# Retention's gates and values: the last additions of each column pair as accumulating transfers, and one more row pair by 7 products

## The chip, the cores and the metric

The kernel runs on one core of one Trainium2 chip. The metric is device time in microseconds of one execution. The core's engines are TensorE (PE, with its weight loads shown apart as PEld), VectorE (DVE), ScalarE (ACT), GpSimd (POOL) and SyncE (SP); SP, ACT and POOL also issue DMA transfers, each in its own queue and in order.

## What is computed

A decoder trunk of two layers, float32, for 256 rows of 2048 features. The first layer is a retention layer followed by a squared-ReLU MLP, the second a latent-attention layer followed by another such MLP. The change touches the retention layer:

```python
def retention(h, w_in, w_out, cos, sin):
    proj = h @ w_in
    q, k, v, gate = jnp.split(proj, [H * dk, 2 * H * dk, 2 * H * dk + H * dv], axis=-1)
    q = apply_rope(...); k = apply_rope(...) * (dk ** -0.5)
    ...
    o = o_intra + o_cross
    o = o * lax.rsqrt(jnp.mean(o * o, axis=-1, keepdims=True) + RMS_EPS)
    return (jax.nn.silu(gate) * o) @ w_out
```

There are 8 heads; a head's q and k are 256 wide, its v and its gate 512 wide. `h` is the normed input. The kernel scales by the norm's gain on the way in and by each row's factor (`r0`) only after the product.

## The kernel before

**Tiles and products.** Every float32 operand is split into a high part and a low part (`split`, lines 180 to 189: a copy on ACT, then a subtraction on DVE), and a product is three matmuls, high by high, high by low and low by high (lines 352 to 354). Weights come in chunks of 128 x 2048 through a pool of three `raw` tiles; their parts go to pools of five `wh` and five `wl` tiles. Activations stand ready as split tiles (`act0`, one for each of 8 pairs of 128 features).

**Row pairs and products.** `gemm_pair` (line 329) makes a 256 x 1024 result from 8 row pairs, one `quad` each (line 280). A quad is a 2 x 2 block product. By 8 products it needs the raw weights' two splits only. By 7 products it also needs sums of the activations (`sums0`, from `with_sums`) and sums of the weights (`us`, three DVE additions at lines 312 to 317), which are split too. `kinds` says which pairs take 7: `SEVEN = (3, 5, 7)` or `FOUR = (3, 5, 6, 7)` (lines 47 and 48). FOUR is in use already in the attention's output product (`wop`).

**After the products.** `pair_out` (line 364) copies six accumulators to SBUF tiles on ACT and adds two more on DVE. One step later `rest` makes two subtractions and hands four pairs of tiles on, whose sums are the blocks of the result: (c11, p1), (c12, v), (c21, u), (c22, p5). `summed` (line 381) adds each pair on DVE (line 385).

**Order.** The program is unrolled, and the order of work around the products is written by hand: `later(n, fn)` puts `fn` off by n chunks, `tick` counts chunks, `need` runs waiting work until a tile exists. A planner then orders each engine's instructions by this priority and by what is ready in its own estimate, and gives out buffers. All 512-wide SBUF tiles that are neither weights nor activations (`f2k`, line 72) share 14 buffers, among them the gates, the values, q and k, the score tiles and the input tiles `x0t`.

**Heads.** For head 1 to 7 (lines 728 to 766) come q (stage `rq`, 2 chunks), k (`rk`, 2 chunks), then gate and value together as one column pair (`rp`, 8 chunks), whose results are taken up during the next head's `rq` and `rk`: `paired` (line 753) adds the pairs, passes the gate through Silu (line 756), and `ret_valued` (line 707) splits the value into vh and vl; `ret_out` (line 656) is put off by one chunk and multiplies scores with values, norms on POOL (lines 161 and 163), multiplies by the gate on DVE (line 672), and transposes y two chunks later. After head 3 and after head 7 a half of the output product follows (`ro`).

**Start.** `first_inputs` (line 571) loads a pair of x's transposed columns, `x0t`, splits it, and for the pairs in SEVEN keeps the tile, scales it again in `sum_up` 9 + c chunks later, and makes the sums of activations from it.

**Other accumulating transfers.** `to_home` (line 143) adds results to DRAM tiles `xh` with transfers issued by POOL (line 148).

Of the kernel before, what the change touches and what calls it, by code (L numbers as in the profile page):

```python
# [15 lines left out]
AF = mybir.ActivationFunctionType  # L16
ALU = mybir.AluOpType
# [19 lines left out]
NT = 2  # L37
S = NT * P
# [8 lines left out]
SEVEN = (3, 5, 7)  # L47
QUERY, FOUR = (3, 4, 6, 7), (3, 5, 6, 7)
PI = math.pi

G_MIX0, G_MLP0, G_KV, G_MIX1, G_MLP1 = 0, 16, 32, 48, 64
# [15 lines left out]
def yoco(ctx: ExitStack, tc: tile.TileContext, a):  # L67
    nc = tc.nc
# [3 lines left out]
    def f2k(shape, name, dtype=F32):  # L72
        return pool.tile([P, *shape], dtype, tag="f2k", bufs=14, name=name)
# [8 lines left out]
    def bank(tag, shape, name):  # L82
        t = psum.tile([P, 512], F32, tag=tag, bufs=4 if tag == "acc" else 2, name=name)
        return shaped(t, shape)

    def two_banks(name):
        return psum.tile([P, 2, 512], F32, tag="at", bufs=1, name=name)

    def act_tile(name, dtype=F32R):

        return pool.tile([P, 2, 2, S], dtype, tag="act", bufs=24, name=name)
# [5 lines left out]
    def later(n, fn):  # L97
        queue.append((clock[0] + n, next(count), fn))
# [6 lines left out]
    def tick():  # L105
        clock[0] += 1
        while queue and min(q[0] for q in queue) <= clock[0]:
            run_first()

    def need(items, n):  # L110
        while len(items) < n:
            run_first()
# [41 lines left out]
    def gain(col):  # L154
        return gains[:, col : col + 1]
# [24 lines left out]
    def split(h, l, src, scale=None):  # L180

        if scale is None:
            nc.scalar.copy(h, src)  # L183
            nc.vector.tensor_tensor(l, src, h.bitcast(F32), op=ALU.subtract)  # L184
        else:
            nc.scalar.activation(h, src, AF.Copy, scale=scale)
            nc.vector.scalar_tensor_tensor(
                l, src, scale, h.bitcast(F32), op0=ALU.mult, op1=ALU.subtract
            )

    def split_act(v, src, scales=(None, None)):
        if scales == (None, None):
            split(v[:, :, 0], v[:, :, 1], src)
        else:
            for j in range(2):
                split(v[:, j, 0], v[:, j, 1], src[:, j], scales[j])
# [132 lines left out]
    def gemm_pair(w, chunk0, act, kinds, name, done):  # L329

        made = {}
        total, count = {}, {}
        for seven in kinds:
            for key in ("c11", "c12", "c21"):
                total[key] = total.get(key, 0) + (1 if seven else 2)
            for key in ("p1", "p5", "p6", "p7") if seven else ("c22", "c22"):
                total[key] = total.get(key, 0) + 1

        def get(key):
            if key not in made:  # L340
                if key in ("p6", "p7"):
                    both = two_banks(f"{name}_p67")
                    made["p6"], made["p7"] = both[:, 0], both[:, 1]
                else:
                    made[key] = bank("tp" if key[0] == "p" else "acc", [512], f"{name}_{key}")
            return made[key]

        def mm(key, lhs, rhs):
            dst, n = get(key), count.get(key, 0)
            count[key] = n + 1  # L350
            (ah, al), (bh, bl) = lhs, rhs
            nc.tensor.matmul(dst, ah, bh, start=n == 0, stop=False)  # L352
            nc.tensor.matmul(dst, ah, bl, start=False, stop=False)  # L353
            nc.tensor.matmul(dst, al, bh, start=False, stop=n == total[key] - 1)  # L354

        for i in range(len(kinds)):
            need(act, i + 1)
            v, more = act[i]
            quad(w, chunk0 + i, (v, more if kinds[i] else None), mm, f"{name}{i}")
            if i == len(kinds) - 1:  # L360
                queue.append((clock[0] + 1, -1, lambda: pair_out(made, name, done)))
            tick()

    def pair_out(c, name, done):

        o = {}
        for key in ("c22", "c12", "c11", "c21", "p1", "p5"):
            o[key] = f2k([512], f"{name}_{key}")
            nc.scalar.copy(o[key], c[key])  # L369
        v, u = (f2k([512], f"{name}_{i}") for i in "vu")  # L370
        nc.vector.tensor_tensor(v, c["p6"], o["p1"], op=ALU.add)
        nc.vector.tensor_tensor(u, c["p7"], v, op=ALU.add)

        def rest():
            nc.vector.tensor_tensor(v, o["p5"], v, op=ALU.subtract)
            nc.vector.tensor_tensor(o["p5"], o["p5"], u, op=ALU.subtract)
            done([[(o["c11"], o["p1"]), (o["c12"], v)], [(o["c21"], u), (o["c22"], o["p5"])]])

        later(1, rest)

    def summed(c):

        for row in c:
            for block in row:
                nc.vector.tensor_tensor(block[0], block[0], block[1], op=ALU.add)
        return [[block[0] for block in row] for row in c]

    def with_sums(blocks, name):

        blocks = blocks.rearrange("p j (t n) -> p (j t) n", t=NT)  # L390
        sums = f2k([4, P], f"{name}_sum")
        nc.vector.tensor_tensor(sums[:, 0:2], blocks[:, 0:2], blocks[:, 1:4:2], op=ALU.subtract)
        nc.vector.tensor_tensor(sums[:, 2], sums[:, 1], blocks[:, 0], op=ALU.subtract)
        nc.vector.tensor_tensor(sums[:, 3], blocks[:, 2], sums[:, 2], op=ALU.add)
        more = act_tile(f"{name}_more")
        split_act(more, sums.rearrange("p (j t) n -> p j (t n)", j=2))
        return more
# [130 lines left out]
    scale = (NOPE + ROPE) ** -0.5  # L528
# [40 lines left out]
    act0, sums0, r0, ret_sc, mla_sc, no_turn = [], [], [], [], [], []  # L569

    def first_inputs(c):

        t = f2k([2, S], f"x0t_{c}")
        nc.sync.dma_start(t, a["xt"][:, 2 * c : 2 * c + 2, :])
        v = act_tile(f"a0_{c}")
        split_act(v, t, [gain(G_MIX0 + 2 * c + j) for j in range(2)])
        act0.append(v)
        sums0.append(None)
        if c in SEVEN:

            def sum_up():
                for j in range(2):
                    nc.scalar.activation(t[:, j], t[:, j], AF.Copy, scale=gain(G_MIX0 + 2 * c + j))
                sums0[c] = with_sums(t, f"a0s_{c}")

            later(9 + c, sum_up)

# [119 lines left out]
    def ret_valued(src, h, s, v, gate):  # L707
        for t in range(NT):
            vh = f2k([512], f"vh{h}{t}", F32R)
            vl = f2k([512], f"vl{h}{t}", F32R)  # L710
            split(vh, vl, src[t], r0[t])
            v.append((vh, vl))
        later(1, lambda: ret_out(h, s, v, gate, halves[h // 4]))
# [14 lines left out]
    for h in range(RH):  # L728
        qk, gate, v, s = [], [], [], []
        if h == 0:  # L730

            def gated(acc, gate=gate):
                src = [f2k([512], f"gate_raw{t}") for t in range(NT)]
                for t in range(NT):
                    nc.scalar.copy(src[t], acc[t])

                def silu():
                    for t in range(NT):
                        g = f2k([512], f"gate0{t}")
                        nc.scalar.activation(g, src[t], AF.Silu, scale=r0[t])  # L740
                        gate.append(g)

                later(8, silu)

            gemm(a["ret_w_gv0"], 0, act0, KD, 512, "rg0", gated, start)
            ret_projected(h, qk, gate, v, s)
            gemm(
                a["ret_w_gv0"], 4, act0, KD, 512, "rv0",
                lambda acc, v=v, s=s, gate=gate: ret_valued(acc, 0, s, v, gate),
            )  # L750
            continue

        def paired(c, h=h, gate=gate, v=v, s=s):
            c = summed(c)
            for t in range(NT):
                nc.scalar.activation(c[t][0], c[t][0], AF.Silu, scale=r0[t])
                gate.append(c[t][0])
            ret_valued([c[t][1] for t in range(NT)], h, s, v, gate)

        ret_projected(h, qk, gate, v, s)  # L760
        if h == RH // 2:
            ret_out_half(0)
        need(r0, NT)
        while None in [sums0[k] for k in SEVEN]:
            run_first()
        gemm_pair(a["ret_w_gv"], (h - 1) * 8, list(zip(act0, sums0)), [k in SEVEN for k in range(8)], f"rp{h}", paired)
    ret_out_half(1)


# [412 lines left out]
```

## Time and profile before

| | |
|---|---|
| median of 3 runs | 2503.48 us (2501.48 to 2504.06) |
| span of the profiled execution | 2497.0 us |
| weight loads on PE, busy | 2075.1 us, 83% |
| ACT busy | 1574.8 us, 63% |
| POOL busy | 252.2 us, 10% |
| transfers of the SP queue (q1) | 471.78 MB, 52.5% of 16 engines' span |
| transfers issued by POOL (q0) | 46.15 MB, 8.9% |

The profiled execution has a span of 2497.0 us from its first instruction to its last; the runs' time contains some more around it. A row of a timeline gives the start in us from the span's start, the duration in us, the engine, the line, the operation, the tiles (out<-in), the shapes and a count; in square brackets stands the idle time before it and what ended it. A row of groups ends with the busy time, the mean ns of one, and the idle time before them with its releasers. Matmuls overlap, so their rows are longer than the steps between them.

### The profile page before, as it was taken

The numbers are of one execution on the slowest core, as the hardware profiler recorded it, in microseconds if no ns is written. First come the engines' busy times: TensorE is split into PE (matmuls) and PEld (weight loads), VectorE is DVE, ScalarE is ACT, GpSimd is POOL, SyncE is SP. The second block draws the span as 40 slices with busy tenths as digits, with TensorE's granted clock in tenths as the row PEclk, the third lists the DMA queues.
The fourth block names the chain that finished last, engine by engine and source line by source line (L and its number), as shares of the span: only waits on it lengthen the run. The fifth ranks groups of instructions, "written<-read, shape, count | busy, mean of one in ns | idle before, by whom it ended". The sixth has DMA issues, their size and how long they took to land.

```text
span 2497.0 us, 31492 instructions
## 1 busy us (share of the span) xinstructions
PE 2471.9 (99%) x11683; PEld 2075.1 (83%) x11683; DVE 2096.7 (84%) x2723; ACT 1574.8 (63%) x2228; POOL 252.2 (10%) x308
## 2 busy tenths in 40 slices
PE   8999999999999999999999999999999999999999
PEld 7788888888888888888888888998888888888887
DVE  7788888888898888889889888776899888898896
ACT  6566555555676657566666767666676566575663
POOL 6300011000010110110110101110010201101100
PEclk9999999999999999999999999999999999999999
DMA  8545568555565685775875555444455956857754
GB/s 290 211 173 202 178 217 246 183 193 196 211 217 189 207 263 186 235 237 186 247 259 191 197 196 189 159 149 163 173 213 203 262 203 213 249 187 233 258 200 165
DMA packets 92825, 519.97 MB, mean 208 GB/s; under 512 B 11009, under 2 KB 12161, under 8 KB 39425
## 3 DMA queue, kind: packets, MB, share of 16 engines
q1 hardware_dynamic: 71280, 471.78, 52.5%
q0 software_dynamic: 21248, 46.15, 8.9%
q8 instruction: 91, 1.49, 0.2%
q14 instruction: 62, 0.50, 0.1%
q10 hardware_dynamic: 144, 0.05, 0.0%
HBM read 478.09 MB, written 39.85 MB: 207 GB/s over the span
## 4 chain that ended last, share of the span: by engine, by line
PE 80%; DVE 10%; DMA 4%; ACT 4%; issue 2%; POOL 1%; ACTq 0%; SPq 0%; DVEq 0%; POOLq 0%
PE u_c L353 7%; PE u_c L354 7%; PE u_c L352 7%; PE d_c L353 4%; PE d_c L354 4%; PE d_c L352 4%; PE rp_c L353 3%; PE rp_c L354 3%; PE rp_c L352 3%; DVE d_wl L184 3%; PE ro_c L352 2%; PE ro_c L353 2%; PE ro_c L354 2%; PE rq_acc L272 2%; PE rk_acc L272 2%; DMA d_raw<-in_mlp_w 2%
## 5 line engine op out<-in xcount | busy, mean ns | idle before, releaser
L184 DVE TENSOR_TENSOR u_wl<-u_raw,u_wh 128x1024 fp32r<-128x1024 f32 (+1 forms) x256 | 280.0, 1124 | 35.8 <-ACT u_wh L183 35.8
L184 DVE TENSOR_TENSOR d_wl<-d_raw,d_wh 128x1024 fp32r<-128x1024 f32 (+1 forms) x256 | 283.4, 1132 | 26.0 <-ACT d_wh L183 25.1
L353 PE MATMUL u_c<-u_wl,n 128*128 128x512 f32 x748 | 291.8, 390 | 1.1 <-DVE u_wl L184 1.0
L352 PE MATMUL u_c<-u_wh,n 128*128 128x512 f32 x748 | 291.3, 391 | 0.0
L354 PE MATMUL u_c<-u_wh,n 128*128 128x512 f32 x748 | 291.3, 389 | 0.0
L183 ACT CAST u_wh<-u_raw 128x1024 fp32r<-128x1024 f32 (+1 forms) x256 | 238.9, 981 | 60.6 <-DMA u_raw<-in_mlp_w 27.2
L183 ACT CAST d_wh<-d_raw 128x1024 fp32r<-128x1024 f32 (+1 forms) x256 | 240.0, 991 | 56.3 <-DMA d_raw<-in_mlp_w 25.1
L353 PE MATMUL d_c<-d_wl,hid 128*128 128x512 f32 x644 | 251.4, 390 | 1.7 <-DVE d_wl L184 1.6
L352 PE MATMUL d_c<-d_wh,hid 128*128 128x512 f32 x644 | 252.1, 391 | 0.0
L354 PE MATMUL d_c<-d_wh,hid 128*128 128x512 f32 x644 | 250.9, 390 | 0.0
L183 ACT CAST u_wh<-u_u 128x1024 fp32r<-128x1024 f32 x92 | 94.2, 1050 | 153.5 <-DVE u_u L317 129.8
L183 ACT CAST d_wh<-d_u 128x1024 fp32r<-128x1024 f32 x84 | 84.9, 1049 | 162.6 <-DVE d_u L317 154.7
L353 PEld LDWEIGHTS u_c<-u_wl,n 128*128 128x128 f32 x748 | 140.5, 188 | 31.1 <-DVE u_wl L184 2.8
L354 PEld LDWEIGHTS u_c<-u_wh,n 128*128 128x128 f32 x748 | 140.4, 188 | 29.2
L352 PEld LDWEIGHTS u_c<-u_wh,n 128*128 128x128 f32 x748 | 140.4, 188 | 28.6
L183 ACT CAST rp_wh<-rp_raw 128x1024 fp32r<-128x1024 f32 x112 | 106.7, 972 | 67.7 <-PE rp_c L354 37.5
L184 DVE TENSOR_TENSOR u_wl<-u_u,u_wh 128x1024 fp32r<-128x1024 f32 x92 | 110.7, 1222 | 43.6 <-ACT u_wh L183 43.5
L353 PEld LDWEIGHTS d_c<-d_wl,hid 128*128 128x128 f32 x644 | 120.9, 188 | 29.0 <-DVE d_wl L184 4.5
L354 PEld LDWEIGHTS d_c<-d_wh,hid 128*128 128x128 f32 x644 | 120.9, 188 | 25.1
L352 PEld LDWEIGHTS d_c<-d_wh,hid 128*128 128x128 f32 x644 | 120.9, 188 | 24.6
L184 DVE TENSOR_TENSOR d_wl<-d_u,d_wh 128x1024 fp32r<-128x1024 f32 x84 | 99.9, 1222 | 35.9 <-ACT d_wh L183 35.9
L148 POOL DMA_DIRECT2D xh<-d_c x48 | 42.1, 1029 | 844.6 <-ACT d_c L369 844.5
(567 smaller groups left out, 6570.0 us busy)
## 6 DMA issues: line engine op xcount, KB each, us to landing
u_raw<-in_mlp_w SPq DMA_DIRECT2D x128, 1024.0 KB, 5.3
d_raw<-in_mlp_w SPq DMA_DIRECT2D x112, 1024.0 KB, 4.9
rp_raw<-in_ret_w_gv SPq DMA_DIRECT2D x56, 1024.0 KB, 4.9
ro_raw<-in_ret_w_out SPq DMA_DIRECT2D x32, 1024.0 KB, 4.9
uq_raw<-in_mla_w_uq SPq DMA_DIRECT2D x24, 768.0 KB, 4.1
rq_raw<-in_ret_w_qk SPq DMA_DIRECT2D x16, 1024.0 KB, 6.6
rk_raw<-in_ret_w_qk SPq DMA_DIRECT2D x16, 1024.0 KB, 4.8
d_raw<-in_mlp_w2t SPq DMA_DIRECT2D x16, 1024.0 KB, 5.1
```

Of the source, the lines that this page charges most:

```text
L148: nc.gpsimd.dma_start(x_home[t][2 * p + j], part, accum_op=ALU.add)
L183: nc.scalar.copy(h, src)
L184: nc.vector.tensor_tensor(l, src, h.bitcast(F32), op=ALU.subtract)
L272: nc.tensor.matmul(acc[f], wh[:, cols], a.rearrange("p i s -> p (i s)"), start=k == 0, stop=k == nk - 1)
L352: nc.tensor.matmul(dst, ah, bh, start=n == 0, stop=False)
L353: nc.tensor.matmul(dst, ah, bl, start=False, stop=False)
L354: nc.tensor.matmul(dst, al, bh, start=False, stop=n == total[key] - 1)
```

## The change

The last additions of a retention head's column pair are issued as four transfers by POOL that accumulate from one SBUF tile into another, in place of four DVE additions; Silu, the split of the values and what follows come one chunk later. In the same stage the row pairs by 7 products are FOUR in place of SEVEN. The sums for these pairs are no longer made from the kept `x0t` tile: `sum_up` loads the columns once more into a tile of its own, for four pairs instead of three.

```diff
-        if c in SEVEN:
+        if c in FOUR:
 
             def sum_up():
+                again = f2k([2, S], f"x0s_{c}")
+                nc.sync.dma_start(again, a["xt"][:, 2 * c : 2 * c + 2, :])
                 for j in range(2):
-                    nc.scalar.activation(t[:, j], t[:, j], AF.Copy, scale=gain(G_MIX0 + 2 * c + j))
-                sums0[c] = with_sums(t, f"a0s_{c}")
+                    nc.scalar.activation(again[:, j], again[:, j], AF.Copy, scale=gain(G_MIX0 + 2 * c + j))
+                sums0[c] = with_sums(again, f"a0s_{c}")
...
         def paired(c, h=h, gate=gate, v=v, s=s):
-            c = summed(c)
-            for t in range(NT):
-                nc.scalar.activation(c[t][0], c[t][0], AF.Silu, scale=r0[t])
-                gate.append(c[t][0])
-            ret_valued([c[t][1] for t in range(NT)], h, s, v, gate)
+            for t, j in ((0, 0), (1, 0), (0, 1), (1, 1)):
+                nc.gpsimd.dma_start(c[t][j][0], c[t][j][1], accum_op=ALU.add)
+
+            def landed():
+                for t in range(NT):
+                    nc.scalar.activation(c[t][0][0], c[t][0][0], AF.Silu, scale=r0[t])
+                    gate.append(c[t][0][0])
+                ret_valued([c[t][1][0] for t in range(NT)], h, s, v, gate)
+
+            later(1, landed)
...
-        while None in [sums0[k] for k in SEVEN]:
+        while None in [sums0[k] for k in FOUR]:
             run_first()
-        gemm_pair(a["ret_w_gv"], (h - 1) * 8, list(zip(act0, sums0)), [k in SEVEN for k in range(8)], f"rp{h}", paired)
+        gemm_pair(a["ret_w_gv"], (h - 1) * 8, list(zip(act0, sums0)), [k in FOUR for k in range(8)], f"rp{h}", paired)
```

## The prediction

> **What bounds the kernel now.** I read the page first, then the timeline of TensorE in one steady stretch, then the busy time of one whole head.
>
> ```profile
> span 2497.0 us, 31492 instructions
> PE 2471.9 (99%) x11683; PEld 2075.1 (83%) x11683; DVE 2096.7 (84%) x2723; ACT 1574.8 (63%) x2228; POOL 252.2 (10%) x308
> PE 80%; DVE 10%; DMA 4%; ACT 4%; issue 2%; POOL 1%; ACTq 0%; SPq 0%; DVEq 0%; POOLq 0%
> ```
>
> ```profile
> 251.96 0.39 PE L352 MATMUL rp_c<-rp_wh,a 128*128 128x512 f32 x1
> ...
> 255.13 0.39 PE L354 MATMUL rp_c<-rp_wh,a 128*128 128x512 f32 x1
> ...
> 213.40:281.80 68.40, 68.40 (x338) 57.74 (x337) 57.42 (x75) 40.36 (x54) 1.83 (x4) 1.00 0.52 187
> ```
>
> TensorE (PE) sets the time: it is busy 99% of the span and carries 80% of the chain. The 0.39 us of a matmul's row is not its price, since the next one starts before it ends. From 251.96 to 255.13 there are 14 steps, so a matmul costs 3.17/14 = 0.227 us. In the second row (one head, from 213.40 us on: its columns are PE, weight loads, DVE, ACT, POOL) PE never stops for 68.40 us, at full clock, while DVE works 57.42 us and ACT 40.36. So matmuls taken away are worth their 0.227 us, and vector work costs nothing as long as DVE stays ahead.
>
> **The change, part by part.** *Matmuls removed.* In each of the seven paired heads, row pair 6 goes from 8 products to 7, and a product is 3 matmuls: 7 x 3 = 21 matmuls x 0.227 = -4.8 us. This is the whole direct gain.
>
> *Vector work added and removed.*
>
> ```profile
> L184 DVE TENSOR_TENSOR rp_wl<-rp_raw,rp_wh 128x1024 fp32r<-128x1024 f32 x91 | 107.7, 1220 | 6.7 <-ACT rp_wh L183 6.2
> L184 DVE TENSOR_TENSOR rp_wl<-rp_u,rp_wh 128x1024 fp32r<-128x1024 f32 x42 | 51.3, 1225 | 25.6 <-ACT rp_wh L183 25.5
> L312 DVE TENSOR_TENSOR rp_u<-rp_raw 128x1024 f32<-128x1024 f32 x21 | 25.6, 1221 | 11.4 <-DMA rp_raw<-in_ret_w_gv 11.4
> L316 DVE TENSOR_TENSOR rp_u<-rp_u,rp_raw 128x512 f32<-128x512 f32 x21 | 14.5, 689 | 0.4
> L317 DVE TENSOR_TENSOR rp_u<-rp_u,rp_raw 128x512 f32<-128x512 f32 x21 | 14.4, 688 | 0.3
> L184 DVE TENSOR_TENSOR rp_wl<-rp_raw,rp_wh 128x512 fp32r<-128x512 f32 x21 | 14.4, 685 | 0.0
> L385 DVE TENSOR_TENSOR rp_c<-rp_c,rp_p 128x512 f32<-128x512 f32 x14 | 9.6, 689 | 1.7 <-ACT rp_p L369 1.7
> ```
>
> A pair by 8 costs DVE 2 x 1.22 = 2.4 us, against 24 x 0.227 = 5.4 us of PE. A pair by 7 costs 1.22 + 0.69 + 2 x 1.22 + 1.22 + 2 x 0.69 = 7.0 us, against 21 x 0.227 = 4.8. So pair 6 adds 4.5 us of DVE a head, and the four L385 additions give 2.8 back: DVE rises by 1.8 us a head to 59.2 of 67.7, still under PE. On average that is free. Not locally: pairs 5, 6 and 7 now stand in a row, 21 us of DVE against 14.3 of PE, and the recovery that pair 6 gave is gone.
>
> The lead that DVE has must cover those 6.7 us. The same order of pairs (3, 5, 6, 7) already runs in this kernel, in wop; its end shows the price:
>
> ```profile
> 212.82 1.23 DVE L184 TENSOR_TENSOR rp_wl<-rp_u,rp_wh 128x1024 fp32r<-128x1024 f32 x1 [0.73 <-ACT rp_wh L183]
> ...
> 218.97 0.39 PE L272 MATMUL rq_acc<-a,rq_wh 128*128 128x512 f32 x1
> ...
> 1801.14 2.36 DVE L184 TENSOR_TENSOR wop_wl<-wop_u,wop_wh 128x1024 fp32r<-128x1024 f32 x2 [1.20 <-ACT wop_wh L183]
> 1803.42 1.29 DVE L461 TENSOR_TENSOR x_wo<-wop_c,x_wo 128x512 f32<-128x512 f32 x2
> 1804.62 1.22 DVE L184 TENSOR_TENSOR u_wl<-u_raw,u_wh 128x1024 fp32r<-128x1024 f32 x1
> ```
>
> ```profile
> 1801.57 0.39 PE L352 MATMUL wop_c<-wop_wh,ot 128*128 128x512 f32 x1
> ...
> 1804.61 1.07 PE L352 MATMUL u_c<-u_wh,n 128*128 128x512 f32 x4
> 1805.90 0.50 PE L353 MATMUL u_c<-u_wl,n 128*128 128x512 f32 x1 [0.23 <-DVE u_wl L184]
> ```
>
> In rp (before) the last split ends at 214.05, 4.9 us before the next stage's first matmul. In wop it ends at 1803.50, only 1.1 us before it, so DVE is 3.8 us later there. The 12 matmuls from 1801.57 to 1804.61 take 3.04 us where 12 x 0.227 = 2.72 would do: 0.3 us lost inside the stage. Behind it four matmuls take 1.29 instead of 0.91 us: 0.4 more, because u_wl stands behind two L461 additions, which rp does not have. So a head loses between 0.3 and 0.7 us. I take 0.35, near the inner loss: 7 x 0.35 = +2.5 us (bounds 2.1 and 4.9).
>
> *Four additions become four accumulating transfers, and what reads them moves one step later.*
>
> ```profile
> 221.86 0.69 DVE L375 TENSOR_TENSOR rp_v<-rp_p,rp_v 128x512 f32<-128x512 f32 x1
> ...
> 223.07 0.69 DVE L376 TENSOR_TENSOR rp_p<-rp_p,rp_u 128x512 f32<-128x512 f32 x1
> ...
> 226.01 0.75 DVE L187 SCALAR_TENSOR_TENSOR vl<-rp_c,n_r,vh 128x512 fp32r<-128x512 f32 x1
> ...
> 225.96 0.72 ACT L186 ACTIVATE vh<-rp_c,n_r 128x512 fp32r<-128x512 f32 x1
> ...
> 230.25 0.39 PE L664 MATMUL o<-vh,sh 128*128 128x512 f32 x1
> 219.31 0.40 PE L272 MATMUL rq_acc<-a,rq_wh 128*128 128x512 f32 x1
> ```
>
> Call the end of rp zero (218.97). The last transfer can start when L376 has run: now 4.8 us after zero. In the changed kernel DVE comes 3.8 us later out of rp, but two L385 leave the path; two rq splits after 1803.50's place (-1.1 + 2.4), two first additions (1.4), a split (1.2) and the two subtractions (1.4) make 5.3. The nearest rows for the transfer itself are accumulations of the same size from the same kind of tile, but into DRAM:
>
> ```profile
> L148 POOL DMA_DIRECT2D xh<-ro_c x4: 857/914/1202, 350.6 to 355.3; - x4
> ...
> DMA to landing us min/median/max: 3.8/6.5/9.7
> ...
> ro_raw<-in_ret_w_out SPq DMA_DIRECT2D x6, 1024.0 KB, 7.7
> ...
> ro_raw<-in_ret_w_out SPq DMA_DIRECT2D x32, 1024.0 KB, 4.9
> ...
> DMA to landing us min/median/max: 7.4/10.5/15.7
> ```
>
> (The last row is xh<-d_p, the fourth and eighth in bursts that share the engines with weight loads.) SBUF to SBUF does not occur in this trace, so it is bounded by 3.8 and 9.7: landed 9.1 to 15.0 after zero. Then vh (0.72) and vl (0.75): 10.6 to 16.5. The reader is ret_out, now one chunk later: it started 11.3 after zero (230.25), and an rk chunk is 16 pairs of matmuls, 219.31 - 218.97 = 0.34 us each, 5.5 us; so 16.8, and the second value tile 6 matmuls later at 18.2. Both bounds leave cover (1.7 to 7.6 us), so I take 0. Waiting behind the landing are ACT's vh with the casts behind it and DVE's vl with the rk splits behind it. Those splits end about 9 us after zero now and are needed from 11.3 on, so a landing at the far bound could cost PE one to two us. POOL issues 28 transfers of about 0.9 us; only ret_out's two small scalings are queued behind them, and they need the landing anyway. Of the last head, y is needed by the seventh row pair of ro; its transposes now come one pair before instead of two, 4.8 us of cover.
>
> Two rules of the Trainium skill, "DMA: Bandwidth & Descriptors": the section on the anatomy of one DMA gives 2.0 us plus bytes/436e3, an estimate of 2.6 us for 256 KB, and by that the cover would be over 8 us; the landings above do not agree under load. The section on queues says that each DMA engine alternates between the queue rows that have work, packet by packet, which speaks against this change; the trace agrees, weight loads land in 7.7 us beside accumulations against 4.9 over all.
>
> *The start.* The scaled x0t tiles were held until sum_up; now they are free after the first split, and four 256 KB reloads enter SP's queue between the rq/rk/rp weights of head 1.
>
> ```profile
> 59.77 1.23 SPq L596 DMA_DIRECT2D x<-in_x  x2
> ...
> 81.41 0.69 DVE L626 TENSOR_TENSOR rq_q<-rq_u,rope_tab 128x512 f32<-128x512 f32 x1 [0.81 <-ACT gate L740]
> ...
> 85.97 1.57 PE L645 MATMUL sc<-rq_q,rk_q 128*128 128x256 f32 x8 [1.61 <-DVE rk_q L629]
> ...
> 80.00:100.00 20.00, 17.86 (x98) 14.97 (x97) 15.77 (x27) 9.97 (x16) 10.16 (x17) 1.00 0.39 145
> ```
>
> rq_q does not read the gate: L626 waited for a buffer of the shared pool of 14, and PE then stood 1.61 us. Three buffers more should loosen that. The reloads meet DMA engines busy 39%, so I cost them at nothing; uncovered, one is a quarter of a weight load, about 1.2 us each. Bounds: -1.6 (wait gone) and +4.8 (all reloads uncovered). I take -1.6, the row that names a mechanism.
>
> **Sum.** -4.8 + 2.5 + 0 - 1.6 = -3.9 us on the span of 2497.0. The median is 2503.48, 6.5 above the span, so I forecast 2503.5 - 3.9 = 2499.6 us. What a measurement can tell from no change is about 0.2%, 5 us, and this lies inside it.
>
> **The rivals.**
>
> *A, the lead holds.* No wop-like loss, because rp starts with idle DVE and rq has no L461. For it: PE stops nowhere in the head shown. Against: wop's pairs are the same ones in the same buffers. -4.8 - 1.6 = -6.4 at full, 2497.1 us.
>
> *B, late landing: the wait moves from DVE to the transfers.* From a landing later than 16.7 after zero (18.2 - 1.5), ret_out stops PE; at 15.7 us of landing, the largest row, it is 5.3 + 15.7 + 1.5 - 18.2 = 4.3 us a head, +30; at a middle landing of 13.4, 2.0 us a head, +14: 2499.6 + 14 = 2513.6. For it: bursts beside weight loads. Against: the first two are ready some 3 us earlier than the last two, and nothing goes through DRAM.
>
> *C, the saving is eaten.* Stage ends at 0.7 us (4.9 in all) and no gain at the start: +0.1, 2503.6 us. The products are gone, but DVE has become the bound at each rp end. For it: wop's second loss. Against: that one stands behind L461.
>
> **How the numbers follow.** Forecast 0.40 (its own range 2497.5 to 2502), A 0.27, B 0.20, C 0.13. A reaches past 0.2% faster; with the fast edge of the forecast, 0.05, faster has 0.32. C is no change, so same is 0.35 + 0.13 = 0.48 less the slow tail of C, 0.03: 0.45. Slower is B and that tail, 0.23. The range goes from 2495.5 (A with the start's other short waits gone too) to 2512, short of B's middle, which leaves out about 2 in 10.
>
> **What would show it.** Row pairs by 7: 21 fewer matmuls. At the end of rp, the last rp_wl split about 1 us ahead of rq's first matmul, not 4.9, and short PE gaps named after rp_wl. L664 about 17 us after the end of rp; if its gap names vl or vh, B is right. rp_c transfers landing within 10 us of issue. L645 at 86 us without its 1.61. The forecast is wrong if rk matmuls wait for rk_wl behind vl, if weight loads stand behind a reload on SP, or if the L620 additions at the end of rk come late behind ret_out's L672 and hold rp's first matmuls.

## The result, and the profile after

| | before | after |
|---|---|---|
| median, same set of runs | 2502.48 us (2498.68 to 2504.06, 4 runs) | 2518.43 us (2517.02 to 2523.21, 4 runs) |
| ratio, 95% interval | 1 | 1.0076 [1.0056, 1.0095] |
| profiled execution, span | 2497.0 us | 2517.1 us |

The changed kernel is slower by 0.8% by the ratio in the table, and by 0.6% (16.0 us) if the two medians are divided; the interval of the ratio holds both. The forecast of 2499.6 us is missed by 19 us, and the time lies above the range, whose end was 2512. From the page of the changed kernel, the busy times and the chain by engine:

```profile
PE 2476.3 (98%) x11662; PEld 2070.2 (82%) x11662; DVE 2106.7 (84%) x2734; ACT 1585.0 (63%) x2245; POOL 283.6 (11%) x336
...
PE 76%; DVE 12%; ACT 5%; DMA 4%; issue 2%; POOL 1%; ACTq 0%; SPq 0%; DVEq 0%; POOLq 0%
```

The 21 matmuls are gone (11683 to 11662). DVE's total hardly moves, and yet PE's share of the chain falls by 4 points, of which DVE takes 2 and ACT 1. Whom PE waited for stands in the view of waits (waiter, its line, whom it waited for; us in total, times, longest), first after, then before:

```profile
PE rp_c L352 <- DVE rk_u L622: 9.7, 6, 2.3
...
PE d_c L353 <- DVE d_wl L184: 4.9, 6, 1.1
...
PE ro_c L352 <- DVE rk_u L622: 3.0, 1, 3.0
...
PE u_c L353 <- DVE u_wl L184: 1.9, 3, 1.3
```

```profile
PE d_c L353 <- DVE d_wl L184: 1.6, 4, 0.5
...
PE u_c L353 <- DVE u_wl L184: 1.0, 2, 0.8
...
PE rp_c L352 <- DVE rk_u L620: 0.5, 1, 0.5
```

So the new wait is not for a transfer, nor for a value tile. It is for rk_u, the DVE additions at the end of rk (L620 before, L622 now), which must read rk's accumulators before rp may write into the same banks. There is one such wait in each of the heads 1 to 7 (head 4's stands ahead of `ro`, hence the second of the rows): two of 0.6 us and five of 1.9 to 3.0, 9.7 + 3.0 = 12.7 us in all, where the kernel before has 0.5. The timeline of PE where rk ends and rp begins, head 6 (the first two rows are the beginnings of rq and of `ret_out`; 519.13 is the end of the rp before, the zero of the prediction's sum):

```profile
519.13 0.61 PE L272 MATMUL rq_acc<-a,rq_wh 128*128 128x512 f32 x2
...
536.41 0.39 PE L666 MATMUL o<-vh,sh 128*128 128x512 f32 x1
...
545.27 0.39 PE L354 MATMUL rp_c<-rp_wh,a 128*128 128x512 f32 x1
547.52 0.50 PE L352 MATMUL rp_c<-rp_wh,a 128*128 128x512 f32 x1 [1.86 <-DVE rk_u L622]
...
548.09 0.61 PE L354 MATMUL rp_c<-rp_wh,a 128*128 128x512 f32 x1
...
551.48 0.42 PE L353 MATMUL rp_c<-rp_wl,a 128*128 128x512 f32 x1
```

The third product should have started at 545.27 + 0.23 = 545.50 and starts at 547.52: 2.0 us lost. Behind that the steps are long: from 548.09 to 551.48 there are 8 in 3.39 us, 0.42 us each instead of 0.227, 3.39 - 1.82 = 1.57 us more (below, under the hardware). Now DVE's timeline over the same place, after and then before:

```profile
537.48 3.49 DVE L184 TENSOR_TENSOR rp_wl<-rp_raw,rp_wh 128x1024 fp32r<-128x1024 f32 x3
...
544.11 0.75 DVE L674 SCALAR_TENSOR_TENSOR y<-o,o_r,rp_c 128x512 f32<-128x512 f32 x1 [1.67 <-ACT rp_wh L183]
544.78 1.22 DVE L184 TENSOR_TENSOR rp_wl<-rp_raw,rp_wh 128x1024 fp32r<-128x1024 f32 x1
545.91 1.22 DVE L312 TENSOR_TENSOR rp_u<-rp_raw 128x1024 f32<-128x1024 f32 x1
547.04 0.75 DVE L622 TENSOR_TENSOR rk_u<-rk_acc,rk_u 128x256 f32<-128x256 f32 x2
```

```profile
525.11 0.75 DVE L672 SCALAR_TENSOR_TENSOR y<-o,o_r,rp_c 128x512 f32<-128x512 f32 x1 [1.66 <-ACT rp_wh L183]
...
532.05 0.78 DVE L620 TENSOR_TENSOR rk_u<-rk_acc,rk_u 128x256 f32<-128x256 f32 x2 [0.57 <-ACT rk_u L619]
```

Before, the second multiplication by the gate (y) is done 6 us ahead of rk_u, and the first rk_u waits 0.57 us for ACT's copy of the accumulator. After, y comes last in the stage: it ends at 544.86. Behind it the planner's order puts a split and an addition for rp, 2.3 us, and only then rk_u. DVE runs back to back from 544.11 on, and PE waits for it. How long it waits hangs on one small step ahead of y, POOL's scaling of one number for each partition, which takes 0.19 us in some heads and up to 2.70 in others (see the last section).

### The profile page after: what moved, and what is told of

Read it like the earlier page. It is cut to its first block, busy times and chain, and to the rows that moved or that the text cites. A ratio compares the mean times of both kernels' runs of the same rounds, so it can differ in the third digit from the quotient of the medians.

```text
span 2517.1 us, 31572 instructions
## 1 busy us (share of the span) xinstructions
PE 2476.3 (98%) x11662; PEld 2070.2 (82%) x11662; DVE 2106.7 (84%) x2734; ACT 1585.0 (63%) x2245; POOL 283.6 (11%) x336
## 4 chain that ended last, share of the span: by engine, by line
PE 76%; DVE 12%; ACT 5%; DMA 4%; issue 2%; POOL 1%; ACTq 0%; SPq 0%; DVEq 0%; POOLq 0%
PE u_c L353 7%; PE u_c L354 7%; PE u_c L352 7%; PE d_c L353 5%; PE d_c L354 5%; PE d_c L352 5%; DVE rp_wl L184 2%; PE rp_c L352 2%; PE rp_c L354 2%; PE rp_c L353 2%; PE ro_c L353 2%; PE ro_c L352 2%; PE ro_c L354 2%; DMA d_raw<-in_mlp_w 2%; PE u_p L352 2%
```

## Where the 20 us are

Between the two profiled executions lie 2517.06 - 2497.05 = 20.0 us. (The medians differ by 16.0: that of the changed kernel lies 1.4 us above its profiled span, that of the kernel before 5.4, so the profiled execution before was a short one.) By three stretches of PE's timeline:

| stretch | before | after | difference |
|---|---|---|---|
| from the start to the first matmul of head 1's rp | 106.94 | 103.16 | -3.8 |
| heads 1 to 7: from there to the first matmul of the second `ro` | 537.51 | 557.34 | +19.8 |
| from there to the end | 1852.59 | 1856.56 | +4.0 |

*Heads 1 to 7.* The waits for rk_u make 12.7 - 0.5 = 12.2 us more. Four of the gaps are followed by steps at half clock; at the 1.57 us worked out above that is 6.3. The fourth pair by 7 products gives 0.6 net (worked out below). 12.2 + 6.3 - 0.6 = 17.9; the other 1.9 us are not traced to a row.

*The start.* Of the 3.8 us, 3.0 stand at the first scores (82.93, was 85.97). But 1.4 of them stand already at head 0's first rq matmul (30.56, was 32.00), well ahead of the first reload, which is issued at 79.89. The other 1.6 are the reload's: the kernel with the reload alone, below, has no gain at the first of these places (32.29) and 1.5 us at the second (84.49).

*The rest.* The change doesn't touch this stretch. In the profiled executions of the twelve kernels of this document it takes 1852.2 to 1856.6 us, with the kernel before near the low end and the changed one at the high end, so its 4.0 us can't be put down to the change. Waits for d_wl and u_wl, 3.3 + 0.9 = 4.2 us longer here, vary in the same way: a kernel below that cures the wait for rk_u has 3.7 and 0.5.

## The experiments

My theory after reading the two traces (theory 1): the step "one chunk later" carries the norm and the gate product of `ret_out` to DVE just ahead of rk_u, and rp's accumulators come free late. Rivals: the load of the fourth pair by 7 on DVE (theory 2), or the transfers themselves (theory 3). The kernel before read 2502.5 us in the set of the result and 2497.5 to 2497.7 in those of the experiments, so only ratios to the kernel before of the same set are compared, and an expectation in us is to be read 5 us lower. The change itself was timed in the first set alone. All in one table, before the single experiments: the ratio with its interval, then the stretch of heads 1 to 7 in the profiled execution, which was 537.5 us before:

| copies added by, and when | three pairs by 7 | four pairs by 7 |
|---|---|---|
| DVE, at once (with the reload of x) | 0.9994 [0.9985, 1.0003]; 539.0 | 1.0038 [1.0026, 1.0051]; 546.1 |
| DVE, readers one chunk later | | 1.0058 [1.0046, 1.007]; 550.0 |
| transfers, readers at once | | 1.0101 [1.0083, 1.012]; 561.0 |
| transfers, readers one chunk later | 1.0052 [1.0037, 1.0067]; 550.5 | 1.0076 [1.0056, 1.0095]; 557.3 (the change) |
| the same, `ret_out` two chunks later | 0.9993 [0.9981, 1.0005]; 537.7 | 0.9999 [0.999, 1.0009]; 537.8 |
| the same, rk freed by ACT alone | 0.9995 [0.9986, 1.0005]; 537.1 | 1.0007 [0.9998, 1.0017]; 538.1 |
| both of these cures | | 1.0009 [1.0, 1.0019]; 541.4 |

**The fourth pair alone.** Additions back on DVE, at once; the reload of x and FOUR stay.

```diff
-            for t, j in ((0, 0), (1, 0), (0, 1), (1, 1)):
-                nc.gpsimd.dma_start(c[t][j][0], c[t][j][1], accum_op=ALU.add)
...
-            later(1, landed)
+            c = summed(c)
+            for t in range(NT):
+                nc.scalar.activation(c[t][0], c[t][0], AF.Silu, scale=r0[t])
+                gate.append(c[t][0])
+            ret_valued([c[t][1] for t in range(NT)], h, s, v, gate)
```

> The changed kernel with the four DVE additions and the old timing back (no transfers, no delay); FOUR and the reload of x stay. Theory 1 (the one-chunk delay puts ret_out's chain of norm and gate in front of the rk_u additions that free rp's accumulators): no stall at the start of rp, second rk_u addition within 1 us after rk's end, time 2498 to 2503 us. Theory 2 (pairs 5, 6, 7 in a row make DVE the bound): still slow, 2510 us or more. Theory 3 (the transfers and their landing): as theory 1, 2498 to 2503.

Measured 1.0038, clearly slower than the kernel before. The expected time of my theory was missed (2506.3 us, against 2493 to 2498) and lies in theory 2's range (2505 or more): FOUR is not near nothing when the additions stay on DVE. What the theory said of the stall holds: PE waits for rk_u in one place, 0.6 us. DVE and then PE in the timeline, at the start of head 6's rq:

```profile
511.06 1.21 DVE L184 TENSOR_TENSOR rq_wl<-rq_raw,rq_wh 128x1024 fp32r<-128x1024 f32 x1
...
514.60 0.68 DVE L385 TENSOR_TENSOR rp_c<-rp_c,rp_p 128x512 f32<-128x512 f32 x1
```

```profile
512.32 0.38 PE L268 MATMUL rq_acc<-a,rq_wl 128*128 128x256 f32 x1 [0.31 <-DVE rq_wl L184]
...
516.16 0.50 PE L666 MATMUL o<-vh,sh 128*128 128x512 f32 x1 [0.33 <-ACT vh L186]
```

DVE comes out of rp late, then owes splits of rq and four L385 additions at once (514.60 is the last of them), and PE stops twice a head. Late by some 4 us, those additions are no longer free. That suggests a use for the change's transfers: beside FOUR they take work from DVE at the point where it is behind.

**The transfers and the delay, without a fourth pair.** The change with SEVEN in all three places; the reload of x stays.

```diff
-        if c in FOUR:
+        if c in SEVEN:
...
-        while None in [sums0[k] for k in FOUR]:
+        while None in [sums0[k] for k in SEVEN]:
...
-        gemm_pair(a["ret_w_gv"], (h - 1) * 8, list(zip(act0, sums0)), [k in FOUR for k in range(8)], f"rp{h}", paired)
+        gemm_pair(a["ret_w_gv"], (h - 1) * 8, list(zip(act0, sums0)), [k in SEVEN for k in range(8)], f"rp{h}", paired)
```

> The changed kernel with SEVEN in place of FOUR: transfers, delay and reload stay, 21 matmuls more. Theory 1: the stall of about 2 us at the start of each rp stays (heads 2 to 6), time 2512 to 2522 us. Theory 2: the loss is gone, about 2500 to 2504 us. Theory 3: 2515 us or more.

Measured 1.0052, inside theory 1's range less 5 us. Without a fourth pair the wait is still there, though only two of the seven are as long as 2 us: those of the heads in which POOL's scaling takes 2.16 and 1.98 us (under 1 us in the others). Its view of waits:

```profile
PE rp_c L352 <- DVE rk_u L622: 7.5, 6, 2.4
```

**The delay alone.** DVE adds the copies as before; only Silu, the split of the values and `ret_out` come one chunk later.

```diff
-            for t, j in ((0, 0), (1, 0), (0, 1), (1, 1)):
-                nc.gpsimd.dma_start(c[t][j][0], c[t][j][1], accum_op=ALU.add)
+            c = summed(c)
...
             later(1, landed)
```

> The changed kernel with the sums made by the four DVE additions at their old place, but Silu, the split of the values and what follows still one chunk later: no accumulating transfer. Theory 1: as slow as the changed kernel, 2512 to 2522 us, with the same gap before rp's third result named after rk_u. Theory 3: 2498 to 2504 us. Theory 2: slower than the changed kernel, since DVE has 19 us more to do.

Measured 1.0058. PE in this kernel's view of waits:

```profile
PE rq_acc L268 <- DVE rq_wl L184: 6.1, 13, 0.6
...
PE rp_c L352 <- DVE rk_u L622: 3.0, 6, 0.6
```

There is no transfer here to wait for, and each rp still waits for rk_u; so the delay is enough to make this wait. But it is 0.5 us a head (0.6 in head 1), not the gap of 2 us that theory 1 expected. In head 6 from `ret_out`'s first matmul to rp's it takes 7.7 us, as in the change, but to rk_u's start 9.25 instead of 10.63: 1.38 less, which is the time of POOL's scaling, 0.19 here and 1.57 there. So the transfers have a part in the length of the wait after all. A likely path, not tested by a run of its own: in the change ACT's first vh of head 6 waits 1.35 us for a landing (at 534.11), the casts behind it come late, and DVE's run of splits then falls on POOL's step. Of the 12.5 us by which heads 1 to 7 are longer than before in this kernel, the wait for rk_u is 3.5, and that in rq (additions that fall on DVE there) 6.1.

**Rk's accumulators freed by ACT alone.** The change, with ACT copying both halves of rk's accumulators, and DVE adding the copies when it comes to it (rq's stay as they are).

```diff
-        for i in range(2):
-            nc.scalar.copy(u[:, i], acc[i][:, S:])
-            nc.vector.tensor_tensor(u[:, i], acc[i][:, 0:S], u[:, i], op=ALU.add)
+        w = f2k([2, S], f"{name}_w")
+        for i in range(2):
+            nc.scalar.copy(u[:, i], acc[i][:, S:])
+            nc.scalar.copy(w[:, i], acc[i][:, 0:S])
+        nc.vector.tensor_tensor(u, w, u, op=ALU.add)
```

> The changed kernel, but rk's accumulators are freed by ACT alone: both halves are copied to SBUF by ACT, and DVE adds the copies. Theory 1: the gap at the start of rp falls from about 2 us to under 1 us, no halved clock behind it, time 2498 to 2506 us. Theories 2 and 3: no gain, 2515 to 2520 us.

Measured 1.0007. The timeline of DVE, same head and place:

```profile
530.31 0.75 DVE L681 SCALAR_TENSOR_TENSOR y<-o,o_r,rp_c 128x512 f32<-128x512 f32 x1 [1.67 <-ACT rp_wh L183]
...
532.11 1.22 DVE L312 TENSOR_TENSOR rp_u<-rp_raw 128x1024 f32<-128x1024 f32 x1
...
533.97 0.69 DVE L625 TENSOR_TENSOR rk_u<-rk_w,rk_u 128x512 f32<-128x512 f32 x1
```

DVE is as late as in the change, its addition even later. But PE no longer depends on it: it stops nowhere between rk and rp, and the time is back at that of the kernel before. The transfers, the late gate product and FOUR are all still in this kernel.

**`ret_out` one chunk later still.** The change, with `ret_out` of heads 1 to 6 put off by two chunks.

```diff
-        later(1, lambda: ret_out(h, s, v, gate, halves[h // 4]))
+        later(2 if h in (1, 2, 3, 4, 5, 6) else 1, lambda: ret_out(h, s, v, gate, halves[h // 4]))
```

> The changed kernel with ret_out of heads 1 to 6 one chunk later still, behind the end of rk. Theory 1 (chain of norm and gate in front of the rk_u additions): rk_u ends within 1.5 us of rk's end again, no gap of 2 us there, ratio to the kernel before 0.998 to 1.002. Rival (DVE is behind there whatever stands in its queue, since rp's pairs in a row left it behind): the gap stays above 1.5 us, ratio above 1.005.

Measured 0.9999: a further delay removes the cost of the first. DVE's timeline:

```profile
527.80 0.75 DVE L622 TENSOR_TENSOR rk_u<-rk_acc,rk_u 128x256 f32<-128x256 f32 x2
...
532.94 0.74 DVE L674 SCALAR_TENSOR_TENSOR y<-o,o_r,rp_c 128x512 f32<-128x512 f32 x1
```

Now rk_u stands ahead of y, with 4 us between them. What mattered was not how late the chain is, but that it fell on the one point where DVE owes PE something.

**Both cures, and the cures with SEVEN.** Four more kernels: the two cures together; each cure with SEVEN; and the kernel before with only the reload of x.

> The changed kernel with both cures: rk's accumulators freed by ACT alone, and ret_out of heads 1 to 6 one chunk later. Theory 1 (one fault, the late additions that free rp's accumulators): each cure alone already removed it, so the two together are worth no more than one, ratio 0.999 to 1.001 against the kernel before, heads of 68.2 to 68.6 us. Rival (each cure leaves a part of the loss that the other takes): the stalls of more than 0.3 us that are left in either trace go too, heads come near 67.7 us, ratio 0.996 to 0.998.

> The kernel of e4 (rk's accumulators freed by ACT) with SEVEN in place of FOUR: it shows what the seventh-product pair is worth once the gap at the start of rp is out of the way. By the prediction's terms (21 matmuls, 4.8 us, less 2.5 us lost where the pairs stand in a row) it is 2.3 us slower than e4, ratio to the kernel before 1.001 to 1.003. If the pairs in a row lose as much as they save, it is as fast as e4 or faster, ratio 0.999 to 1.001.

> The changed kernel with ret_out of heads 1 to 6 one chunk later, and SEVEN in place of FOUR. If a fourth pair by 7 products is worth nothing beside the pairs in a row (as the pair of runs with ACT-freed accumulators says), this is equal to the kernel with FOUR, ratio 0.999 to 1.001. If FOUR earns its 21 matmuls once rk's end is out of the way (prediction's own sum, 2.3 us net), this is slower than it by 0.1 per cent, 1.001.

> The kernel before with the reload of x for sum_up alone (SEVEN, DVE additions, no delay). If the shared buffers held the start up, as the prediction has it, the first scores come 2 to 4 us earlier and the time is 2 to 4 us under the kernel before (ratio 0.9985 to 0.999). If the gain at the start is made elsewhere in the change, no difference.

The two cures together read 1.0009, no better than one alone, as one fault would have it; its trace has no wait for rk_u, but PE's waits for the score tile `st` and for rp_wh add up to 3.8 us in it, against 1.2 with rk freed by ACT alone, so it is a weak test. With SEVEN the cures read 0.9995 and 0.9993, with FOUR 1.0007 and 0.9999: the intervals overlap, and nowhere does FOUR come out ahead, in the stretch of heads 1 to 7 neither. The reload of x alone reads 0.9994; its interval holds 1 as well as the 1.6 us (0.9994) that the prediction gave it. Its first scores come 1.5 us earlier (84.49, was 85.97): about the gain of the prediction, and less than the 2 to 4 us expected of this run. None of the kernels is faster than the kernel before by more than the intervals allow. In the view of waits of the kernel with SEVEN and the later `ret_out`, the row that was 7.5 without this edit:

```profile
PE rp_c L352 <- DVE rk_u L622: 0.5, 1, 0.5
```

Where the 21 matmuls went is seen at the end of rp in PE's timeline, with rk freed by ACT; first with FOUR, then with SEVEN:

```profile
502.27 0.80 PE L352 MATMUL rp_p<-rp_wh,a0s_more 128*128 128x512 f32 x2
...
503.23 0.39 PE L354 MATMUL rp_c<-rp_wh,a 128*128 128x512 f32 x1
...
505.08 0.62 PE L272 MATMUL rq_acc<-a,rq_wh 128*128 128x512 f32 x2
505.76 0.61 PE L268 MATMUL rq_acc<-a,rq_wl 128*128 128x256 f32 x3
506.21 0.40 PE L272 MATMUL rq_acc<-a,rq_wh 128*128 128x512 f32 x1
```

```profile
503.66 0.39 PE L272 MATMUL rq_acc<-a,rq_wh 128*128 128x512 f32 x1
503.89 0.28 PE L268 MATMUL rq_acc<-a,rq_wl 128*128 128x256 f32 x1
504.00 0.40 PE L272 MATMUL rq_acc<-a,rq_wh 128*128 128x512 f32 x1
504.24 0.40 PE L268 MATMUL rq_acc<-a,rq_wl 128*128 128x256 f32 x2
504.47 0.40 PE L272 MATMUL rq_acc<-a,rq_wh 128*128 128x512 f32 x1
```

The first two wide and three narrow matmuls of rq take 506.21 - 505.08 = 1.13 us with FOUR and 504.47 - 503.66 = 0.81 with SEVEN: 0.32 lost. Inside rp the three from 502.27 to 503.23 (two in the first row, one left out) take 0.96 where 3 x 0.227 = 0.68 would do: 0.28 lost. (The changed kernel's rows at the same two places in head 6 take 1.14 and 0.96.) Together 0.60 of the 3 x 0.227 = 0.68 us that a head saves, so 7 x 0.08 = 0.6 us remain of 4.8.

**Transfers without the delay.** The change, with Silu, the values and `ret_out` taken up at once.

```diff
-            later(1, landed)
+            landed()
```

> The changed kernel without the delay: transfers and FOUR stay, but Silu, the split of the values and ret_out take their old places in the order. Theory 1: the gap at the start of rp goes; but the values are needed 11 us after the end of rp and land at 13, so PE waits some 3 to 4 us in ret_out in each head: ratio 1.006 to 1.010. Rival (the landing is early enough, the delay alone did the harm): ratio 0.998 to 1.002.

Measured 1.0101, just past the far end of what theory 1 expected. PE's waits for the value's high and low part, and the one for rk_u; and ACT's timeline in head 6, where vh waits for the transfers:

```profile
PE o L666 <- ACT vh L186: 12.1, 9, 2.5
...
PE o L667 <- DVE vl L187: 2.9, 11, 0.3
...
PE rp_c L352 <- DVE rk_u L622: 0.6, 1, 0.6
```

```profile
532.98 0.72 ACT L186 ACTIVATE vh<-rp_c,n_r 128x512 fp32r<-128x512 f32 x1 [2.50 <-DMA rp_c<-rp_v]
```

Now PE does wait for the landing, as the prediction's rival B had it, and the wait for rk_u has gone with the delay, though the transfers and FOUR are still there. So the transfers need the delay, and the delay brings the other wait.

## Why the prediction was wrong

**What held.** PE has 21 fewer matmuls. The last split of rp now ends 1.1 us ahead of rq's first matmul, as worked out from wop (was 4.9). The row (DVE, after), and the transfers' summary:

```profile
515.67 2.36 DVE L184 TENSOR_TENSOR rp_wl<-rp_u,rp_wh 128x1024 fp32r<-128x1024 f32 x2 [1.20 <-ACT rp_wh L183]
```

```profile
DMA to landing us min/median/max: 3.3/6.9/9.6
```

515.67 + 2.36 = 518.03, against 519.13. The transfers land in 3.3 to 9.6 us, inside the bounds of 3.8 to 9.7 but for the lower edge. `ret_out` starts 536.41 - 519.13 = 17.3 us after zero (forecast 16.8), and no gap there names vh or vl, so rival B, whose price was nearest to the result, did not happen: its time came from another mechanism. The start gained 3.0 us at the first scores; 1.6 of them belong to the reload, as forecast, and the kernel with the reload alone has 1.5. The other 1.4 were there before it. PE, after:

```profile
82.93 1.57 PE L647 MATMUL sc<-rq_q,rk_q 128*128 128x256 f32 x8 [0.69 <-DVE rk_q L631]
```

**The step that failed** is in the part on the transfers: "Both bounds leave cover (1.7 to 7.6 us), so I take 0". That cover was worked out for the readers of the landed tiles, up to `ret_out`'s first matmuls. But `ret_out` was moved as well, and with it all that follows from it: two norms on ACT and POOL and two gate products y on DVE, in DVE's order. Zero plus 11.3 became zero plus 17.3 for its start. In the trace of before it takes 7.4 us from there to the end of the second y (in head 6 from 518.48, where o starts 11.3 after its zero of 507.19, to 525.11 + 0.75). That alone would have put y's end at 17.3 + 7.4 = 24.7, beside rk's end (rp's first matmul is five steps ahead of the row at 545.27, 25.0 after zero). Measured: 544.86 - 519.13 = 25.7. One more us comes from POOL's scaling, which took 1.57 us instead of 0.54. Then the two jobs ahead of rk_u, 2.3 us. The queue behind the moved step was asked of ACT, of DVE's vl and of POOL, and not of y. The prediction's last sentence names this mechanism among the ways to be wrong, with L620 behind L672, but it was given no price and no chance. With the rows of before it would have been a rival of 1 us a head: y's end at 24.7, 2.3 for the two jobs and 0.4 for the first addition make 27.4, and rp's third product is due at 26.4. That is 7 us, still inside the range. What carried the time beyond the range is the scaling: it takes 0.19 to 0.64 us in all heads of the kernel before, and 1.57 to 2.70 in five heads of the changed one, where it stands behind a run of DVE's splits; without that these five waits would be some 9 us shorter in all, and the half clock follows none of the short ones. So the term put at 0 measured 12.2 us of waits and some 6.3 of half clock.

**The size that was off.** FOUR's loss at each stage end was put at 0.35 us, near the inner loss alone, and measured 0.60 (0.28 inside rp and 0.32 in rq). Both halves of wop's price applied, and the bounds of 0.3 to 0.7 held. The reason for taking the low end, that rq has no additions like L461 ahead of its splits, did not hold: DVE is late there anyway. That is 7 x 0.25 = 1.8 us of the miss; the direct saving is then almost all eaten, as rival C said, for another reason.

## What to carry to other kernels

When a step is put off, follow everything it issues down to each engine's queue, and compare the new place of the last of it with the next instruction there that frees a buffer for the bound engine; 5 us of delay with "cover" for its readers cost PE 2 to 3 us in five of seven heads. Follow its small steps too: one of 0.19 us on POOL took up to 2.70 behind a run of DVE's splits. Accumulators that the bound engine needs back can be read by an engine that has no long jobs in front, and the addition made from copies; here that took the cost of the wait away. And look where DVE enters the next stage before counting matmuls as saved by more vector work: here it came 3.8 us later, and 0.60 of 0.68 us came back as short gaps.

## What the runs showed of the hardware

**Half clock after a short stop.** Three windows of the changed kernel, each around one gap (columns as in the prediction; the granted clock is the third number from the end):

```profile
244.00:254.00 10.00, 7.74 (x39) 6.19 (x38) 9.12 (x15) 4.71 (x7) 0.75 (x2) 1.00 0.41 148
...
470.00:480.00 10.00, 7.77 (x29) 5.96 (x29) 8.33 (x14) 4.16 (x7) 0.74 (x2) 0.83 0.52 197
543.00:553.00 10.00, 8.14 (x30) 6.27 (x30) 8.89 (x14) 3.69 (x7) 0.74 (x2) 0.83 0.43 157
```

A mean of 0.83 over 10 us is 3.4 us at half clock: 10 x (1 - 0.83) x 2. A stop of some 2 us can cost another 1.6 us that way. Of the five long gaps (1.86 to 2.98 us) four are followed by it (at 176, 319, 475 and 547 us). At 248 us the gap is no shorter than three of these, and the clock stays at 1.00:

```profile
248.29 0.50 PE L352 MATMUL rp_c<-rp_wh,a 128*128 128x512 f32 x1 [2.26 <-DVE rk_u L622]
```

The Trainium skill, "TensorE: Matmul & The Clock Gate", section "What's actually happening", says that the clock goes to half after an idle window of about 3.4 us and that this window runs freely. The length of the slow stretch and its halved steps agree; that 2 us of idle time are enough in four places of five is less than the page's condition, and that it depends on where the gap falls fits a free-running window, though no run here moved a gap on purpose to show it. One place speaks for it: in the attention layer, which the change doesn't touch, PE has the same gap in both kernels, 1.88 us before and 1.87 after (ended at 1640.24 and 1661.53); in the 10 us behind it (1641 to 1651, and 1661 to 1671) the granted clock is 0.83 before and 1.00 after.

**A small POOL operation behind DVE's splits.** POOL's timeline, after, in head 6 and head 4; the operation is one number for each partition:

```profile
539.45 1.57 POOL L161 TENSOR_SCALAR o_m<-so 128x1 f32<-128x1 f32 x1 [13.74 <-ACT o_sq L178]
...
543.25 0.19 POOL L161 TENSOR_SCALAR o_m<-so 128x1 f32<-128x1 f32 x1 [1.59 <-ACT o_sq L178]
```

```profile
310.62 2.70 POOL L161 TENSOR_SCALAR o_m<-so 128x1 f32<-128x1 f32 x1 [13.59 <-ACT o_sq L178]
```

The same operation takes 0.19 or 1.57 or 2.70 us. The long ones end when DVE's run of splits ends: 539.45 + 1.57 = 541.02, and the three splits from 537.48 end at 540.97; 310.62 + 2.70 = 313.32, and three splits end at 313.26. The Trainium skill, "SBUF — State Buffer", section "SBUF: two separate sides", says that a DVE instruction with two SBUF inputs and a GpSimd instruction that reads SBUF exclude each other for a whole instruction. The rows agree, and show more: POOL did not get in between two of DVE's splits, but waited for the whole run.

This step sets the length of PE's wait, since y, and behind it rk_u, come after it. In heads 2 to 7 of the changed kernel the first scaling takes 1.86, 1.78, 2.70, 1.94, 1.57 and 0.25 us, and PE's wait for rk_u 2.15, 2.26, 2.98, 2.23, 1.86 and 0.60. With the delay alone the scaling is 0.19 in these six heads, and the wait 0.47 to 0.53.
